# Thresholded attention on one core: scores in seven single PSUM banks, 512-column exponentials and copies on two engines, and an order of steps from a table

## The chip, the cores and the metric

The kernel runs on 1 core of one Trainium2 chip. The metric is device microseconds of one execution. PE, DVE, ACT, POOL and SP are the names of the core's engines as in the profile (TensorE, VectorE, ScalarE, GpSimd, SyncE); PEld is PE's loading of weights. PSUM is the memory into which PE writes; it has eight banks of 512 f32 columns on each of the 128 partitions.

## What is computed

The reference is attention with a cut (shapes: batch 8, heads 12, sequence 512, dimension 64, f32; threshold 0.1):

```
scores  = einsum('bhqd,bhkd->bhqk', Q, K) * scale
weights = exp(scores - max(scores)); weights /= sum(weights) + 1e-10
weights = where(weights > threshold, weights, 0)
weights /= sum(weights) + 1e-10
out     = einsum('bhqk,bhkd->bhqd', weights, V)
```

With these inputs most queries have no weight above 0.1, so their output row is zero, and the few others have one, so that their output row is one row of V.

## The kernel before, in words

The 96 heads are taken as 48 pairs (`hp`), two pairs make a unit (`q` or `u`, 24 of them; the first is split into two half units), and four units make a group (`x`, 6 of them).

**The coarse part** finds candidate queries. For each unit SP's queue loads K (`load_k`, L370 and after) and Q (`load_q`, L375), and writes zeros to the unit's part of the output (`do_zero`, L598). POOL scales Q and casts it to f16 (`do_qcast`, L385). PE transposes K in f32 (`do_ktr`, L395) and Q in f16 (`do_qtr`, L406) into PSUM. ACT copies K transposed out (`do_kev`, L413), POOL casts that to f16 (`do_kh`, L418), and DVE copies Q transposed out (`do_qev`, L422). Then, for each pair and each of four blocks `t` of 128 keys, PE makes scores of both heads, 128 x 1024 (`do_sc`, L438): this is a score step, of which there are 192. One engine, ACT with an exponential (L447) or DVE with an integer trick that stands for one (L449), turns them into an `e` tile (`do_ex`). PE sums `e` and a power of it over the keys into one accumulator bank, `acc` (`do_g`, L469; two such steps for a pair), and adds a bound from the sizes of the inputs, which DVE prepares (`do_bits`, L428; `do_size`, L476).

**The exact part** of a group, once all its sums are in `acc`: DVE empties it (`do_evac`, L479), PE and DVE flag the candidate queries and give each a slot (`do_test` to `do_oh`, L485 to L505), PE makes the indices (`do_idx`, L515), POOL gathers up to 128 rows of Q by an indirect DMA (`do_gather`, L529), and splits them (`do_split`, L536). PE transposes the rows (`do_xtr`, L541) and multiplies them with K in f32 (`do_xqk`, L555), ACT takes the exponential with its sum (`do_xexp`, L561), DVE finds the key above the cut (`do_xkeep`, L570), POOL gathers that row of V (`do_gv`, L585) and scatters it to the output (`do_scatter`, L592). The exact part of a group runs amid the coarse part of the next one; that of the last group has none behind it. A check at the end (L707 to L733) decides whether a slow branch is taken; it isn't with these inputs.

**PSUM** is cut into three tiles `two` of two banks each, for scores and transposes, one bank `acc`, and one bank `one` for the exact part. A `two` tile is held from PE's first matmul into it to the end of the instruction that empties it.

**The order.** Every step is recorded in a `Plan` (L11) with the engines that may do it, a cost, a latency after it, a priority, and the buffers it takes and gives back. `Plan.order` (L24) puts the steps one after the other on a modelled clock, and with that settles which of ACT and DVE does each exponential and which buffer each step uses. The steps are then issued in this order (L724), and `keep` holds the instructions of an engine in it. Each engine works through its own queue in order, and so does each engine that issues DMAs: an instruction that waits holds up all behind it. Two such entries, for the scores and the exponential:

```
add(("sc", hp, t), {"PE": 0.23}, 0.2, [("qev", u), ("kh", u)], g - 3, ...
add(("ex", hp, t), {"ACT": 0.95, "DVE": 1.14}, 0.15, [("sc", hp, t)], g, ...
```

Of the kernel before, what the change touches and what calls it, by code (L numbers as in the profile page):

```python
# [3 lines left out]

# [5 lines left out]

class Plan:  # L11
# [3 lines left out]
    SWITCH = 0.06  # L15

    def __init__(self, pools):
        self.ops, self.ids, self.pools = [], {}, pools

    def add(self, name, engs, lat, deps, prio, fn, takes=(), gives=(), mode=None):  # L20
        self.ids[name] = len(self.ops)
        self.ops.append((name, engs, lat, list(deps), prio, fn, list(takes), list(gives), mode))

    def order(self):  # L24
        ops, ids = self.ops, self.ids
        n = len(ops)
        succ, need, ready_at = [[] for _ in range(n)], [0] * n, [0.0] * n
        for i, op in enumerate(ops):
            for d in op[3]:
                succ[ids[d]].append(i)  # L30
                need[i] += 1
        engines = {e for op in ops for e in op[1]}
        free_at = {e: 0.0 for e in engines}
        ready = {e: set() for e in engines}
        pe_mode = None
        idle = {p: [(0.0, b) for b in range(k)] for p, k in self.pools.items()}
        held = {}

        def offer(i):
            for e in ops[i][1]:  # L40
                ready[e].add(i)

        for i in range(n):
            if need[i] == 0:
                offer(i)

        def begin(i, e):
            t = max(ready_at[i], free_at[e])
            if e == "PE" and ops[i][8] and pe_mode and ops[i][8] != pe_mode:
                t = max(ready_at[i], free_at[e] + self.SWITCH)  # L50
            want = {}
            for pool, _ in ops[i][6]:
                want[pool] = want.get(pool, 0) + 1
            for pool, k in want.items():
                if len(idle[pool]) < k:
                    return None
                t = max(t, sorted(idle[pool])[k - 1][0])
            return t

        out = []  # L60
        while len(out) < n:
            best = None
            for e in sorted(engines):
                at = [(begin(i, e), i) for i in sorted(ready[e])]
                at = [(t, i) for t, i in at if t is not None]
                if not at:
                    continue
                t0 = min(t for t, _ in at)
                prio, t, i = min((ops[i][4], t, i) for t, i in at if t <= t0 + 0.06)
                if best is None or (t, prio) < best[:2]:  # L70
                    best = (t, prio, i, e)
            assert best is not None, "the plan is stuck"
            t, _, i, e = best
            name, engs, lat, deps, prio, fn, takes, gives, mode = ops[i]
            for x in engs:
                ready[x].discard(i)
            free_at[e] = t + engs[e]
            if e == "PE" and mode:
                pe_mode = mode
            for pool, key in takes:  # L80
                b = min(idle[pool])
                idle[pool].remove(b)
                held[pool, key] = b[1]
            for pool, key in gives:
                idle[pool].append((t + engs[e] + lat, held[pool, key]))
            out.append((t, i, e))
            for j in succ[i]:
                ready_at[j] = max(ready_at[j], t + engs[e] + lat)
                need[j] -= 1
                if need[j] == 0:  # L90
                    offer(j)
# [7 lines left out]
def kernel(  # L99
# [21 lines left out]
    GP = 8  # L121
# [235 lines left out]
    def at(pool, key):  # L357
        return plan.held[pool, key]
# [450 lines left out]
```

## Time and profile before

| | us |
|---|---|
| median of 3 runs (lowest, highest) | 229.33 (223.48, 230.46) |
| the profiled execution | 225.0 |
| its span, first to last instruction | 223.3 |
| outside the span | 1.7 |
| busy: PE, DVE, ACT, POOL | 172.4, 158.9, 135.8, 83.9 |
| mean granted TensorE clock | 0.94 of full speed |

The span is one profiled execution. Busy times leave out waiting. A row of groups reads: line, engine, operation, output tile, input tile, shapes, count, then busy us in all and the mean ns of one, then the idle time just before these instructions and what ended most of it. In a row of the order of time the first number is the start in us, the second the time that the (merged) instructions took, and square brackets hold the idle time just before and its releaser. A matmul row's time holds its way through the array, so rows of PE that follow closely overlap. The names `two`, `one`, `qk` and so on are the kernel's tiles with the buffer number left out.

### The profile page before, as it was taken

The page shows a single profiled execution, that of the slowest core. Times are in us where ns is not written, and L with a number is a line of the kernel's source. Part 1 is how long each engine was busy: PE and PEld are TensorE (multiplying, and loading weights), DVE is VectorE, ACT ScalarE, POOL GpSimd, SP SyncE. Part 2 cuts the span into 40 slices and gives each one's busy share as a digit, 9 for nine tenths or more (in the row PEclk, how much of TensorE's full clock was granted, in tenths as well). Part 3 has the DMA queues.
Part 4 walks back from the last instruction along what each step waited for, and adds up shares of the span by engine and source line. Part 5 has one row for each costly group of instructions (what it writes and reads, how often), then busy time and mean ns, then how long its engine had stood idle before and what let it go on. Part 6 is the DMA issues. An engine that isn't in the chain of part 4 may idle for free. (4 is left out here: it accounts for less than half of the span.)

```text
span 223.3 us, 5606 instructions
## 1 busy us (share of the span) xinstructions
PE 172.4 (77%) x2240; PEld 68.4 (31%) x2240; DVE 158.9 (71%) x246; ACT 135.8 (61%) x147; POOL 83.9 (38%) x130
## 2 busy tenths in 40 slices
PE   1498997985989996985898986798987998993330
PEld 0233333341233341331334432334432343222100
DVE  6259987983478897696497797487797897796030
ACT  2366886763478875575466676467677678780010
POOL 7644324462066415334236143246155403130211
PEclk9999999997699999999699999799999999999585
DMA  5999999899659898485785676684687000000000
GB/s 122 237 281 308 281 288 266 232 304 267 166 122 273 241 254 224 156 220 129 211 240 121 203 188 179 211 244 117 205 262 297 3 3 6 3 1 1 6 1 12
DMA packets 67438, 38.43 MB, mean 172 GB/s; under 512 B 51880, under 2 KB 64240, under 8 KB 67408
## 3 DMA queue, kind: packets, MB, share of 16 engines
q1 hardware_dynamic: 66832, 37.76, 60.6%
q8 instruction: 19, 0.31, 0.6%
q0 software_dynamic: 576, 0.27, 0.6%
q14 instruction: 11, 0.09, 0.1%
HBM read 25.56 MB, written 12.78 MB: 172 GB/s over the span
## 5 line engine op out<-in xcount | busy, mean ns | idle before, releaser
L447 ACT ACTIVATE e<-two 128x1024 f16<-128x1024 f32 x107 | 108.0, 1025 | 50.4 <-PE two L438 48.7
L449 DVE TENSOR_SCALAR e<-two 128x1024 int16<-128x1024 f32 x85 | 102.7, 1221 | 29.0 <-PE two L438 28.6
L438 PE MATMUL two<-qk 64*128 64x512 f16 x384 | 70.8, 398 | 21.3 <-ACT e L447 9.1
L469 PE MATMUL acc<-e,w_sum 128*32 128x512 f16 x384 | 59.1, 397 | 0.4 <-DVE e L449 0.4
L469 PE MATMUL acc<-e,w_pow 128*32 128x512 bf16 x384 | 59.1, 397 | 0.0
L385 POOL TENSOR_SCALAR qh<-q 128x512 f16<-128x512 f32 x48 | 30.7, 640 | 55.7 <-issue 29.7
L438 PEld LDWEIGHTS <-qk 64*128 64x128 f16 x384 | 20.0, 95 | 67.8 <-issue 57.4
L366 POOL CAST qk<-kt 128x1024 f16<-128x1024 f32 (+1 forms) x25 | 26.2, 1046 | 15.8 <-ACT kt L362 14.9
L362 ACT COPY kt<-two 128x1024 f32<-128x1024 f32 (+1 forms) x25 | 24.4, 977 | 7.5 <-PE two L395 7.5
L395 PE MATMUL two<-identity_f,k 64*128 64x64 f32 x384 | 18.7, 242 | 9.1 <-DMA k<-in_K_dram 7.1
L395 PEld LDWEIGHTS two<-identity_f,k 64*128 64x128 f32 x384 | 16.0, 152 | 17.5 <-issue 5.6
L469 PEld LDWEIGHTS <-w_sum 128*32 128x32 f16 x384 | 12.3, 96 | 22.5 <-issue 18.9
L364 DVE COPY qk<-two 128x1024 f16<-128x1024 f16 (+1 forms) x25 | 16.5, 660 | 3.6 <-PE two L406 3.6
L428 DVE TENSOR_SCALAR v<-qk 128x1024 int32<-128x1024 int32 x24 | 17.9, 745 | 0.2
L555 PE MATMUL one<-kt,xq 128*32 128x512 f32 x96 | 14.7, 742 | 0.4 <-ACT xq L362 0.4
L529 POOL DMA_INDIRECT qs<-in_Q_dram,idx x6 | 6.8, 1127 | 21.6 <-DVE ix L524 21.5
L592 POOL DMA_INDIRECT out_dram<-vr,idx x6 | 6.2, 1028 | 21.6 <-PE two L438 6.1
L469 PEld LDWEIGHTS <-w_pow 128*32 128x32 bf16 x384 | 12.2, 96 | 0.0
L566 DVE TENSOR_SCALAR sums<-sums 128x1 f32<-128x1 f32 x6 | 0.9, 152 | 14.9 <-ACT xe L561 14.9
L585 POOL DMA_INDIRECT vr<-in_V_dram,idx x6 | 6.5, 1076 | 12.9 <-DVE oks L716 6.5
L406 PEld LDWEIGHTS <-qh 64*128 64x128 f16 x384 | 9.5, 98 | 5.6 <-issue 3.3
L406 PE MATMUL two<-identity_h,qh 64*128 64x64 f16 x384 | 10.3, 194 | 0.5 <-DVE e L449 0.3
(88 smaller groups left out, 81.9 us busy)
## 6 DMA issues: line engine op xcount, KB each, us to landing
k<-in_K_dram SPq DMA_DIRECT2D x96, 128.0 KB, 4.1
out_dram<-zero SPq DMA_DIRECT2D x24, 512.0 KB, 5.1
q<-in_Q_dram SPq DMA_DIRECT2D x23, 512.0 KB, 5.2
q<-in_Q_dram SPq DMA_DIRECT2D x2, 256.0 KB, 4.3
qs<-in_Q_dram,idx POOLq DMA_INDIRECT x6, 3.0
vr<-in_V_dram,idx POOLq DMA_INDIRECT x6, 3.5
out_dram<-vr,idx POOLq DMA_INDIRECT x6, 2.8
```

Of the source, the lines that this page charges most:

```text
L362: keep(nc.scalar.copy(dst, src))
L364: keep(nc.vector.tensor_copy(dst, src))
L366: keep(nc.gpsimd.tensor_copy(dst, src))
L385: keep(nc.gpsimd.tensor_scalar(dst, src, ALPHA, 1.0, op0=ALU.mult, op1=ALU.mult))
L395: keep(nc.tensor.matmul(dst[:, i, c:c + D], lhsT=src[ps, n0 + n, r, :], rhs=identity_f32[ps, ps], is_transpose=True, start=True, stop=True))
L406: keep(nc.tensor.matmul(dst[:, i, :].bitcast(f16)[:, c:c + D], lhsT=src[ps, n0 + n, r, :], rhs=identity_h[ps, ps], is_transpose=True, star ...
L428: keep(nc.vector.tensor_scalar(v_b[at("v", q)][:].rearrange("p a n c -> p (a n c)").bitcast(i32), qk_b[at("qk", q)][:].rearrange("p a n c ...
L438: keep(nc.tensor.matmul(dst[:, h, :], lhsT=qk[ps, 1, n, t * P:(t + 1) * P], rhs=qk[ps, 0, n, :], start=True, stop=True))
L447: keep(nc.scalar.activation(dst, src, ACTF.Exp, scale=math.log(2.0) / 1024.0, bias=exp_bias))
L449: keep(nc.vector.tensor_scalar(dst.bitcast(i16), src, EXP_BIAS * 1024.0, 0.0, op0=ALU.add, op1=ALU.max))
L469: keep(nc.tensor.matmul(dst[32 * j:32 * j + 32, :], lhsT=w, rhs=rhs, **turn(x, j)))
L555: keep(nc.tensor.matmul(one[at("one", ("xs", x))][32 * b:32 * b + 32, :], lhsT=xq[:, a * P + 32 * b:a * P + 32 * b + 32], rhs=kt_b[at("kt" ...
```

## The change

- PSUM is now seven single banks `bank` (pool `bk`) and `acc`. A score step, and a transpose of K or Q, takes two of the seven, one for each of its halves, and each half is given back by itself. The exact part's steps take one of the seven; its own bank `one` is gone.
- The exponential of a score step is two instructions of 512 columns, one for each head (`do_ex(eng, hp, t, h)`), and either engine may do either half. `do_g` picks its weights for each half by the engine that made it (`kind[hp, t, h]`).
- The copies of K transposed and of Q transposed are also two halves each, and each half may be done by ACT or DVE. Before, K's were all ACT's and Q's all DVE's. For the first half unit ACT and DVE also write the f16 keys straight from PSUM; POOL's cast does it for the others, as before.
- There are 14 `e` tiles instead of 12.
- `Plan.order` and all costs, latencies and priorities are gone. `Plan.run` issues the steps by a table of 1136 entries, each the number of a step, a letter for its engine, and the buffers that it takes.
- Q's first block is loaded through ACT's queue; all other loads stay on SP's.
- The last exact part has the same steps as before.

The diff, cut to its core:

```diff
+ORDER = """
+13A2 12S3 0G 11D 6G 5G 1D 38S 8G 10D 37S 7G 9G 64S2 14G1 2G 20P0.1 15P2.3 3G 18A3 16D9 4G 19A 21D 17A 22D 65S1
...
+    def run(self, table):
+        done = set()
+        for token in table.split():
+            no, eng, at = re.fullmatch(r"(\d+)([A-Za-z])(.*)", token).groups()
+            name, engs, deps, fn, takes, gives = self.ops[int(no)]
...
+            for pool, key, count in takes:
+                self.held[pool, key], got = got[:count], got[count:]
+            assert not got
+            fn(self.ENGINES[eng])
...
-    pools = {"two": 3, "acc": 1, "one": 1, "k": 4, "q": 3, "qh": 2, "kt": 10, "qk": 4, "v": 3, "e": 12,
+    pools = {"bk": 7, "k": 4, "q": 3, "qh": 2, "kt": 10, "qk": 4, "v": 3, "e": 14,
...
-    two = [psum.tile([P, 2, SO * P], f32, name=f"two{i}") for i in range(pools["two"])]
-    acc = [psum.tile([P, SO * P], f32, name=f"acc{i}") for i in range(pools["acc"])]
-    one = [psum.tile([P, SO * P], f32, name=f"one{i}") for i in range(pools["one"])]
+    bank = [psum.tile([P, SO * P], f32, name=f"bank{i}") for i in range(pools["bk"])]
+    acc = psum.tile([P, SO * P], f32, name="acc")
...
+        queue = nc.scalar if u == units[0] else nc.sync
...
-    def do_kev(eng, u):
+    def do_kev(eng, u, i):
         q, n0, k = u
-        src = two[at("two", ("ktr", u))][:, :, 0:k * SO * D].rearrange("p i (x c) -> p i x c", c=D)
-        copy(eng, halves(kt_b[at("kt", q)], n0, k), src)
+        src = bank_at(("kp", u), i)[:, 0:k * SO * D].rearrange("p (x c) -> p x c", c=D)
+        copy(eng, side(kt_b[at("kt", q)], n0, k, i), src)
...
-    def do_ex(eng, hp, t):
-        src = two[at("two", ("sc", hp, t))][:].rearrange("p h c -> p (h c)")
-        dst = e_b[at("e", (hp, t))][:].rearrange("p h c -> p (h c)")
+    def do_ex(eng, hp, t, h):
+        src, dst = bank_at(("sc", hp, t), h)[:], e_b[at("e", (hp, t))][:, h, :]
...
-                w = (w_sum, w_pow)[j // 2][kind[hp, t]][:, 31 - m:63 - m]
+                w = (w_sum, w_pow)[j // 2][kind[hp, t, j % 2]][:, 31 - m:63 - m]
...
-        add(("kev", u), {"ACT": 0.1 + 0.43 * k}, 0.15, [("ktr", u)], g0 - 9, lambda e, u=u: do_kev(e, u),
+            add(("kev", u, i), "ACT DVE", [("ktr", u)], lambda e, u=u, i=i: do_kev(e, u, i),
...
-        add(("qev", u), {"DVE": 0.05 + 0.28 * k}, 0.15, [("qtr", u), ("kh", u)], g0 - 7, lambda e, u=u: do_qev(e, u),
+            add(("qev", u, i), "DVE ACT", [("qtr", u)] + keys_of[:1], lambda e, u=u, i=i: do_qev(e, u, i),
...
-    for step, eng in plan.order():
-        step(eng)
+    plan.run(ORDER)
```

How the order moves, at three places. The number behind a tile's name is its buffer; the one behind the underscore only identifies the tensor.

ACT amid group 1, before: `two0` to `two2` are the three PSUM tiles, and `e` the output of an exponential.

```order
L447 ACTIVATE e1_144<-two2_114 128x1024
L362 COPY kt7_133<-two1_113 128x2x8x64
L447 ACTIVATE e3_146<-two1_113 128x1024
L447 ACTIVATE e5_148<-two1_113 128x1024
L447 ACTIVATE e7_150<-two1_113 128x1024
L362 COPY kt8_134<-two0_112 128x2x8x64
L447 ACTIVATE e9_152<-two2_114 128x1024
```

ACT at a like place in the order of the change:

```order
L467 ACTIVATE e7_153<-bank5_117 128x512
L467 ACTIVATE e6_152<-bank3_115 128x512
L467 ACTIVATE e3_149<-bank1_113 128x512
L467 ACTIVATE e2_148<-bank6_118 128x512
L467 ACTIVATE e2_148<-bank5_117 128x512
L467 ACTIVATE e1_147<-bank3_115 128x512
L467 ACTIVATE e1_147<-bank0_112 128x512
L467 ACTIVATE e0_146<-bank4_116 128x512
```

Before, four instructions in a row empty `two1`; now a bank comes back to ACT at the earliest some rows later, and DVE empties others in between.

POOL around the gather of V rows (`vr`, from V) and the scatter (`out`) of group 2, before: `qh` is a Q cast, `qk` a key cast, x2 two instructions.

```order
L366 CAST qk3_139<-kt5_131 128x1024
L585 DMA vr2_175<-in_V_dram,idx2_164 128x64
L592 DMA out_0_dram<-vr2_175,idx2_164 24576x64
L385 TENSOR_SCALAR qh0_124<-q0_121 128x512 x2
L366 CAST qk0_136<-kt6_132 128x1024
```

The same place in the change, and then the same of group 1:

```order
L403 TENSOR_SCALAR qh1_128<-q2_126 128x512 x2
L604 DMA vr0_178<-in_V_dram,idx0_167 128x64
L383 CAST qk2_141<-kt2_131 128x1024
L611 DMA out_0_dram<-vr0_178,idx0_167 24576x64
L403 TENSOR_SCALAR qh0_127<-q1_125 128x512 x2
L383 CAST qk1_140<-kt9_138 128x1024
```

```order
L604 DMA vr1_179<-in_V_dram,idx1_168 128x64
L611 DMA out_0_dram<-vr1_179,idx1_168 16384x64
L403 TENSOR_SCALAR qh1_128<-q0_124 128x512
L383 CAST qk2_141<-kt6_135 128x1024
L403 TENSOR_SCALAR qh1_128<-q0_124 128x512
L403 TENSOR_SCALAR qh0_127<-q2_126 128x512 x2
```

A key cast has moved in between the gather and its scatter in group 2 (the same in group 3; in group 0 two casts); in group 1 the scatter still follows its gather, as all of groups 1 to 4 did before.

POOL at the start, before: `row_no` is a constant of the exact part, `key_i` one of its key numbers; the test constants stand ahead of these rows.

```order
L292 CAST row_no_105<-row_i_104 128x8
L385 TENSOR_SCALAR qh0_124<-q0_121 128x512
L366 CAST qk0_136<-kt0_126 128x512
L299 IOTA key_i_106 128x512
L385 TENSOR_SCALAR qh0_124<-q0_121 128x512
```

In the change:

```order
L307 CAST row_no_105<-row_i_104 128x8
L318 CAST key_no_107<-key_i_106 128x512
L403 TENSOR_SCALAR qh1_128<-q2_126 128x512
L253 MEMSET test_f_96 128x48
L256 AFFINE_SELECT test_f_96<-test_f_96 128x8 x2
```

The first Q cast now has the key numbers ahead of it and the test constants behind it, and no key cast of the first half unit follows it.

More of the change, by code (lines that the diff above doesn't have):

```diff
@@ L206, with const @@
     later = {}
-    def const(name, t):
+    def const(name):
         def wrap(fn):
-            later[name] = (t, fn)
+            later[name] = fn
             return fn
```

423 lines of the change are left out of this document (212 added, 211 removed).

## The prediction

> **What bounds the kernel now.** I read the busy times by stage first. The three stages are the start (to the first score matmul), the body, and the exact step of the last group, which has nothing left to hide behind; below them stand one steady stretch and the three worst ones. Columns: window, length, busy us and instructions of PE, PE's weight loads, DVE, ACT and POOL, the granted clock, the DMA share, GB/s.
>
> ```profile
> 0.00:9.26 9.26, 1.60 (x25) 1.34 (x26) 4.12 (x32) 2.46 (x3) 6.66 (x36) 1.00 0.67 164
> 9.26:202.34 193.08, 165.22 (x2177) 65.11 (x2177) 149.80 (x195) 132.41 (x141) 73.76 (x91) 0.96 0.68 191
> 202.34:223.30 20.96, 5.61 (x39) 1.97 (x39) 5.02 (x19) 0.96 (x3) 3.50 (x4) 0.68 0.02 5
> 20.00:40.00 20.00, 17.74 (x261) 7.05 (x260) 17.33 (x19) 15.90 (x17) 6.87 (x10) 1.00 1.03 282
> 50.00:60.00 10.00, 7.11 (x43) 1.62 (x42) 3.40 (x5) 4.13 (x6) 1.78 (x4) 0.66 0.92 246
> 104.00:112.00 8.00, 4.94 (x66) 2.03 (x64) 3.66 (x5) 3.66 (x4) 3.37 (x5) 0.79 0.56 161
> 138.00:146.00 8.00, 5.41 (x68) 2.29 (x68) 4.11 (x5) 3.98 (x4) 3.43 (x6) 0.79 0.55 171
> ```
>
> The span is 9.3 + 193.1 + 21.0 = 223.3 us. In the body DVE and ACT together work 149.8 + 132.4 = 282.2 us, 141.1 each, 73% of the time. Between 20 and 40 us they do (17.33 + 15.90) / 20 = 1.66 us of work per us. By that rate the last three rows hold 4.5, 4.4 and 4.9 us of work in 10, 8 and 8 us: **three holes** that lose 5.5 + 3.6 + 3.1 = 12.2 us. The other 180.9 us of the body leave each of the two engines 180.9 - 141.1 = 39.8 us idle. What they wait for stands in the table of waits (us in total, times, longest):
>
> ```profile
> ACT e L447 <- PE two L438: 48.7, 69, 3.9
> DVE e L449 <- PE two L438: 28.6, 42, 2.8
> ```
>
> Both wait for scores. Two different reasons show in the order of time. The first, on ACT:
>
> ```profile
> 61.34 1.01 ACT L362 COPY kt<-two 128x1024 f32<-128x1024 f32 x1
> 62.89 1.02 ACT L447 ACTIVATE e<-two 128x1024 f16<-128x1024 f32 x1 [0.54 <-PE two L438]
> 64.45 1.02 ACT L447 ACTIVATE e<-two 128x1024 f16<-128x1024 f32 x1 [0.54 <-PE two L438]
> 66.01 1.02 ACT L447 ACTIVATE e<-two 128x1024 f16<-128x1024 f32 x1 [0.54 <-PE two L438]
> ```
>
> These are rows 40 to 43 of ACT's order, and all four read two1. PE can't refill the tile before ACT has left it, so each costs 1.02 us of work and a **round trip of 0.54 us**. The second reason, a hole, starts on POOL (the last row is PE's):
>
> ```profile
> 96.39 1.09 POOL L585 DMA_INDIRECT vr<-in_V_dram,idx  x1 [0.65 <-DMA k<-in_K_dram]
> 103.59 1.02 POOL L592 DMA_INDIRECT out_dram<-vr,idx  x1 [6.10 <-PE two L438]
> 104.68 1.31 POOL L385 TENSOR_SCALAR qh<-q 128x512 f16<-128x512 f32 x2
> 106.06 1.04 POOL L366 CAST qk<-kt 128x1024 f16<-128x1024 f32 x1
> 107.15 0.39 PE L438 MATMUL two<-qk 64*128 64x512 f16 x2 [3.06 <-POOL qk L366]
> ```
>
> The scatter sits 6.1 us at the head of POOL's queue. Behind it stand a Q cast and the key cast that PE's next scores need, so PE idles 3.06 us. The releaser that the row names is PE work; the gather of V rows just ahead, which the scatter writes out, is the likelier one.
>
> **The change part by part. Shorter instructions.** By these rows a half costs more than half:
>
> ```profile
> L447 ACT ACTIVATE e<-two 128x1024 f16<-128x1024 f32 x107 | 108.0, 1025 | 50.4 <-PE two L438 48.7 <-issue 0.7 <-DVE marks L489 0.2
> L449 DVE TENSOR_SCALAR e<-two 128x1024 int16<-128x1024 f32 x85 | 102.7, 1221 | 29.0 <-PE two L438 28.6
> L362 ACT COPY kt<-two 128x1024 f32<-128x1024 f32 x23 | 23.3, 1011 | 1.7 <-PE two L395 1.7
> L362 ACT COPY kt<-two 128x512 f32<-128x512 f32 x2 | 1.2, 587 | 5.8 <-PE two L395 5.8
> L364 DVE COPY qk<-two 128x1024 f16<-128x1024 f16 x23 | 15.7, 681 | 0.0
> L364 DVE COPY qk<-two 128x512 f16<-128x512 f16 x2 | 0.8, 425 | 3.6 <-PE two L406 3.6
> L489 DVE TENSOR_TENSOR marks<-one,limits 128x192 bf16<-128x192 f32 x6 | 2.1, 351 | 0.6 <-PE one L485 0.4
> L501 DVE TENSOR_TENSOR keys<-one,marks 128x64 bf16<-128x64 f32 x6 | 1.3, 217 | 0.5 <-PE one L497 0.5
> ```
>
> On ACT, 512 columns are worth 1.011 - 0.587 = 0.424 us, so a half exponential is 1.025 - 0.424 = 0.601. On DVE a column from PSUM in f32 takes (351 - 217) / 128 = 1.047 ns, 512 of them 0.536, so a half is 1.221 - 0.536 = 0.685. The built order has 231 halves on ACT and 153 on DVE: 138.8 + 104.8 = 243.6 us against 108.0 + 102.7 = 210.7 before, **+32.9 us**. The key copies: 24.5 us before; now 29 halves on ACT at 0.587, 17 on DVE at 0.685 (an f32 read, costed as the exponential), and the first two units' six quarter-size copies at about 0.4: 31.0, +6.5. The Q copies: 16.5 us before; now 29 halves on DVE at 0.425, 17 on ACT at 0.587, four small ones 1.3: 23.6, +7.1. Together +46.5 us; about 1 of it falls before the first scores, so the body holds 282.2 + 45.5 = 327.7, **164 us per engine** instead of 141. Nothing hides this: both engines are the ones that everything waits for. Its lower bound is about 160, if halves in a row overlap by some 0.02 us each.
>
> [...]
>
> **Seven single banks.** In the order before, 66 of the 242 instructions by which ACT and DVE empty score and transpose tiles read the same buffer as the last such instruction on their engine (37 and 29); in the new order it is 4 of 486. At 0.54 us, 62 x 0.54 = 33.5 us go, **16.7 per engine**. How much of the other idle time stays isn't shown by any row: at most all, 39.8 - 16.7 = 23.1; at least, I put 5. I take it from the steadiest stretch: from 20 to 40 us the two idle (2.67 + 4.10) / 2 = 3.4 of 20, which over 180.9 is 30.7; less 16.7 leaves **14**. The exact step's small matmuls lose their own bank and now hold one of the seven; fourteen e tiles instead of twelve cost no time.
>
> **The order on POOL.** From group 1 on, key casts mostly stand 7 to 11 score steps ahead of their first use (two of them 3 and 4), where they stood 3 to 6 ahead, and in three of the four groups with work behind them a cast stands between the row gather and its scatter, before in one. At 180 / 192 = 0.94 us per score step, 8 steps are 7.5 us, more than the 6.1 that the scatter sat. Only in group 1 does the scatter still follow its gather at once, with half a Q cast and the key cast behind it: 1.09 + 6.1 + 1.02 + 0.66 + 1.04 = 9.9 us against 7.5, so up to 2.4 late. In group 0 the row transpose gets some 5 us of ACT and DVE work behind the gather instead of 2 to 3. Of 12.2 us of holes I keep **1.5** (bounds 0 and 12.2). SP's queue keeps its bytes and puts the zero writes later; in 180 us the body would move 191 x 193.1 / 180 = 205 GB/s, below the 282 of 20 to 40 us.
>
> **The start.**
>
> ```profile
> 2.18 0.61 SPq L377 DMA_DIRECT2D q<-in_Q_dram  x1
> 5.51 0.62 POOL L385 TENSOR_SCALAR qh<-q 128x512 f16<-128x512 f32 x1 [0.42 <-DMA q<-in_Q_dram]
> 7.75 0.69 PE L395 MATMUL two<-identity_f,k 64*128 64x64 f32 x8 [2.54 <-DMA k<-in_K_dram]
> 8.20 0.45 PE L406 MATMUL two<-identity_h,qh 64*128 64x64 f16 x8
> ```
>
> Q's first block lands 3.3 us after its issue. On ACT's queue it is issued about 1.4 us earlier, at 0.8, so it lands near 4.1; POOL's constants ahead of the cast then end near 4.6 (1.65 us of test constants move behind it, 1.18 of key numbers ahead). PE no longer puts the second K block ahead of the first Q transposes: cast to 5.2, Q transposes to 5.7, K transposes to 6.4, copies to about 7.5. First scores at **7.6** instead of 9.26; at 8.4 if the load lands no earlier. ACT issues this one DMA ahead of its table load and has nothing else to do then.
>
> **Sum.** 7.6 + (164 + 14 + 1.5) + 21.0 = 208.1 us of span. The last group's steps are the same, so 21.0 stays. The profiled execution took 225.0 us, 1.7 more than its span: **209.8, so 210 us**. That execution lies near the fast end of the three runs (223.48 to 230.46, median 229.33); a change under 2% is about what a measurement of this kernel can't tell from none.
>
> **The rivals.** (1) *PE sets the pace.* It is busy 165.2 us in the body and gets the same matmuls; from 20 to 40 us it is at 17.74 of 20. If the waits outside the round trips are PE's, all 23.1 stay: 7.6 + 188.6 + 22.7 = 219. Against it: PE waited only 9.1 us for ACT to free a tile:
>
> ```profile
> PE two L438 <- ACT e L447: 9.1, 14, 1.0
> ```
>
> which says that PE was rarely held up, so this rival is a real one. (2) *The holes stay*, since POOL still waits in order for its gathers: 7.6 + (164 + 14 + 12.2) + 22.7 = 220.5. (3) *PE's clock falls in the body.*
>
> ```profile
> 108.00:110.00 2.00, 2.00 (x26) 1.22 (x26) 1.48 (x2) 0.98 (x2) 0.00 (x0) 0.50 1.01 325
> 142.00:144.00 2.00, 2.00 (x26) 1.01 (x22) 1.24 (x2) 1.52 (x2) 0.00 (x0) 0.50 0.98 358
> ```
>
> At half clock ACT and DVE got 5.22 / 4 = 1.31 us of work per us, 79% of 1.66. If PE pauses for the two slower engines so often that a quarter of the body, 45 us, runs so, that is 12 us more: 222. Against it: PE's pauses from 20 to 40 us left the clock at 1.00, and the drops shown follow idle stretches of about 3 us. [...] (4) *Slower: the fixed cost decides.* If ACT and DVE, with every piece half as long, keep the busy share of the body outside its holes, 141.1 / 180.9 = 78%, because each piece still ends in a wait on PE, the body is 164 / 0.78 + 1.5 = 212 and the time 242. It is slower by 2% from a body of 199, that is when 35 of the 39.8 us of waits come back. For it: 244 more PSUM reads, each with its own wait. Against it: the 66 round trips counted above.
>
> **How the numbers follow.** Forecast 0.50, PE's pace 0.17, holes 0.13, clock 0.06, fixed cost 0.14. Low end: 5 us of waits and no hole, 7.6 + 169 + 22.7 = 199, put at 200. High end 224, which takes in the first three rivals; what is left out is rival 4 and a little below. Faster by over 2%: the forecast, rival 1 and a third of rivals 2 and 3, 0.74; slower 0.14; the rest 0.12.
>
> **What would show it.** Right: half exponentials near 0.60 and 0.69 us; waits of ACT and DVE for scores at some 30 us in total, not 77; first scores before 8 us; no stretch of 8 us with under 5 us of work on each of the two; clock 1.00 from 10 to 190 us; the tail again 21 us. Wrong: a body above 190 us, from waits that stay at over 23 us per engine, or a hole behind a scatter.

## The result, and the profile after

Before: 227.46 us median of four runs (223.48 to 230.46). After: **203.80 us** (202.29 to 204.83, four runs). The ratio is **0.907, 95% interval 0.894 to 0.920**. Ratios not said to be on medians compare only executions within 1.5% of their kernel's fastest, so they differ a little from ratios of the medians (203.80 / 227.46 = 0.896). The forecast was 210 us, in a range of 200 to 224. The sum came out 6 us high, but three of its terms were off by 4 to 17 us and happened to cancel.

The stages of the profiled execution after (204.83 us, span 203.1), cut as in the prediction, then the steady stretch and the four stretches with least work. Columns: window, length, busy us and instructions of PE, PEld, DVE, ACT and POOL, granted clock, DMA share, GB/s.

```profile
0.00:7.91 7.91, 0.88 (x17) 0.80 (x18) 4.38 (x34) 2.21 (x4) 6.60 (x35) 1.00 0.70 176
7.91:180.89 172.98, 158.38 (x2185) 64.99 (x2184) 149.63 (x286) 144.84 (x291) 76.41 (x91) 0.96 0.76 214
180.89:203.10 22.21, 6.06 (x39) 1.92 (x39) 5.02 (x19) 0.95 (x3) 3.83 (x5) 0.57 0.02 5
20.00:40.00 20.00, 18.62 (x287) 7.86 (x286) 19.10 (x35) 19.30 (x39) 8.17 (x11) 1.00 0.97 261
48.00:56.00 8.00, 6.32 (x65) 1.92 (x66) 3.00 (x6) 3.20 (x9) 1.64 (x3) 0.79 1.03 269
64.00:72.00 8.00, 5.61 (x74) 2.15 (x74) 4.44 (x9) 4.73 (x10) 4.61 (x6) 0.79 1.05 281
136.00:144.00 8.00, 5.33 (x97) 2.35 (x95) 5.06 (x12) 5.99 (x12) 3.39 (x4) 0.95 0.95 339
144.00:152.00 8.00, 6.47 (x55) 2.19 (x57) 3.98 (x8) 2.69 (x6) 2.17 (x3) 0.62 0.36 144
```

Read it in the prediction's order. In the body DVE and ACT work 149.63 + 144.84 = 294.5 us, **147.2 each**; before it was 141.1, and 164 was forecast. The steady stretch gives (19.10 + 19.30) / 20 = 1.92 us of work per us, where before had 1.66. At that rate the four stretches below lose 4.8 + 3.2 + 2.2 + 4.5 = 14.7 us, and one more at 96 to 104 us (13.13 us of work in 8) loses 1.2: **15.9 us of holes**, not 1.5. The rest of the body leaves each engine 172.98 - 15.9 - 147.2 = **9.9 us of other waits**, where 14 were forecast. The start is 7.91 (forecast 7.6) and the tail 22.2 (21.0). The differences, -16.8 + 14.4 - 4.1 + 0.3 + 1.2 = -5.0, are those between the forecast span of 208.1 and the measured 203.1. How the idle time is shared between holes and other waits hangs on the rate: by before's 1.66, which the prediction used, the same five stretches lose 12.2 us, as much as before's holes did, and 13.6 are other waits.

The groups of exponentials, and the waits for scores (us in total, times, longest):

```profile
L467 ACT ACTIVATE e<-bank 128x512 f16<-128x512 f32 x231 | 121.8, 622 | 16.6 <-PE bank L459 15.7
L469 DVE TENSOR_SCALAR e<-bank 128x512 int16<-128x512 f32 x153 | 97.6, 682 | 5.8 <-PE bank L459 5.3
```

```profile
ACT e L467 <- PE bank L459: 15.7, 20, 4.4
DVE e L469 <- PE bank L459: 5.3, 6, 1.7
PE bank L560 <- POOL qb L555: 11.0, 4, 4.3
```

The waits fell from 48.7 + 28.6 to 15.7 + 5.3 us. And the group rows hold a trap: on ACT 231 x 0.622 = 143.7 us, but the busy time is 121.8; on DVE 153 x 0.682 = 104.3 against 97.6. The busy time counts each moment once, so instructions that follow each other **overlap**. In the order of time, first after, then before; columns: start, length of the run of instructions, and its count behind the x:

```profile
174.44 5.73 ACT L467 ACTIVATE e<-bank 128x512 f16<-128x512 f32 x11
176.79 3.28 DVE L469 TENSOR_SCALAR e<-bank 128x512 int16<-128x512 f32 x5
```

```profile
193.57 4.00 ACT L447 ACTIVATE e<-two 128x1024 f16<-128x1024 f32 x4 [0.30 <-PE two L438]
196.04 4.77 DVE L449 TENSOR_SCALAR e<-two 128x1024 int16<-128x1024 f32 x4 [0.24 <-PE two L438]
```

In these runs a half takes 5.73 / 11 = 0.521 us on ACT and 0.656 on DVE, though each shows 0.622 and 0.682. Two halves (1.04 and 1.31) cost little more than one whole (1.00 and 1.19). The runs still hold short waits: record by record in the traces, where the next starts with no wait, the medians from one start to the next are 0.48 and 0.60 for a half (after), 0.92 and 1.14 for a whole (before).

The worst hole, at 141 to 151 us, and what leads to it, on POOL, PE and ACT (the number in brackets is the idle time just ahead of the row):

```profile
137.19 1.12 POOL L548 DMA_INDIRECT qs<-in_Q_dram,idx  x1 [2.75 <-DVE ix L543]
145.07 0.40 POOL L555 TENSOR_TENSOR qb<-qs,ix 128x128 f32<-128x128 f32 x1 [4.27 <-DMA qs<-in_Q_dram,idx]
145.53 0.47 PE L560 MATMUL bank<-identity_f,qb 128*128 128x128 f32 x1 [4.20 <-POOL qb L555]
146.64 1.58 ACT L467 ACTIVATE e<-bank 128x512 f16<-128x512 f32 x3 [4.42 <-PE bank L459]
```

```profile
136.41 5.49 SPq L618 DMA_DIRECT2D out_dram<-zero  x5
```

```profile
148.00:150.00 2.00, 2.00 (x16) 0.51 (x12) 1.92 (x4) 0.22 (x1) 0.00 (x0) 0.50 0.02 4
DMA to landing us min/median/max: 2.6/4.3/7.8
```

A gather of query rows is issued at 137.2 and its rows are there at 145.0, 7.8 us later (the slowest of six, last line); SP issues five writes of zeros from 136.4 to 141.9. POOL's split, PE's transpose and ACT stand one behind the other, and PE comes back at half clock (0.50 at 148 to 150 us). The 16 f32 matmuls of the exact part then take 3.24 us; at 89 us, with the clock at 1.00, they took 1.92:

```profile
147.32 3.24 PE L574 MATMUL bank<-kt,xq 128*32 128x512 f32 x16
89.00 1.92 PE L574 MATMUL bank<-kt,xq 128*32 128x512 f32 x16
```

The hole at 48 us is of the same kind: PE's transpose stands behind a gather of query rows that took 5.9 us. Those at 64 and 96 us are of the kind that the prediction described: POOL's scatter stands behind a gather of V rows, landed after 6.6 us (58.2 to 64.8) and 4.7 (93.2 to 97.8). In the first of them PE's next transposes wait for the Q cast behind the scatter:

```profile
49.68 0.33 PE L560 MATMUL bank<-identity_f,qb 128*128 128x128 f32 x1 [1.86 <-POOL qb L555]
65.03 1.10 POOL L611 DMA_INDIRECT out_dram<-vr,idx  x1 [2.85 <-DMA k<-in_K_dram]
66.88 0.29 PE L424 MATMUL bank<-identity_h,qh 64*128 64x64 f16 x8 [1.82 <-POOL qh L403]
98.73 1.02 POOL L611 DMA_INDIRECT out_dram<-vr,idx  x1 [4.45 <-PE bank L459]
```

### The profile page after: what moved, and what is told of

Read it like the earlier page. It is cut to its first block, busy times and chain, and to the rows that moved or that the text cites. A ratio compares the mean times of both kernels' runs of the same rounds, so it can differ in the third digit from the quotient of the medians.

```text
span 203.1 us, 5841 instructions
## 1 busy us (share of the span) xinstructions
PE 165.3 (81%) x2240; PEld 67.7 (33%) x2240; DVE 159.0 (78%) x339; ACT 148.0 (73%) x298; POOL 86.8 (43%) x129
## 5 line engine op out<-in xcount | busy, mean ns | idle before, releaser
L467 ACT ACTIVATE e<-bank 128x512 f16<-128x512 f32 x231 | 121.8, 622 | 16.6 <-PE bank L459 15.7
L469 DVE TENSOR_SCALAR e<-bank 128x512 int16<-128x512 f32 x153 | 97.6, 682 | 5.8 <-PE bank L459 5.3
L459 PE MATMUL bank<-qk 64*128 64x512 f16 x384 | 66.9, 392 | 4.8 <-DVE qk L381 1.3
L383 POOL CAST qk<-kt 128x1024 f16<-128x1024 f32 (+1 forms) x24 | 25.7, 1073 | 33.0 <-ACT kt L379 15.9
L488 PEld LDWEIGHTS <-w_sum 128*32 128x32 f16 x384 | 14.1, 96 | 27.9 <-issue 23.1
L413 PE MATMUL bank<-identity_f,k 64*128 64x64 f32 x384 | 18.8, 238 | 0.5 <-ACT e L467 0.5
L413 PEld LDWEIGHTS bank<-identity_f,k 64*128 64x128 f32 x384 | 16.3, 148 | 6.5 <-DVE e L469 2.4
L379 ACT COPY kt<-bank 128x512 f32<-128x512 f32 (+1 forms) x30 | 17.3, 601 | 1.3 <-PE bank L413 1.1
L574 PE MATMUL bank<-kt,xq 128*32 128x512 f32 x96 | 16.3, 811 | 0.4 <-ACT xq L379 0.4
L381 DVE COPY kt<-bank 128x512 f32<-128x512 f32 (+1 forms) x20 | 12.6, 643 | 3.7 <-ACT qk L379 2.0
L611 POOL DMA_INDIRECT out_dram<-vr,idx x6 | 6.3, 1044 | 16.8 <-PE bank L459 5.7
L381 DVE COPY qk<-bank 128x512 f16<-128x512 f16 (+1 forms) x31 | 11.9, 406 | 1.9 <-PE bank L424 1.5
L424 PEld LDWEIGHTS <-qh 64*128 64x128 f16 x384 | 8.2, 96 | 13.5 <-POOL qh L403 9.5
L379 ACT COPY qk<-bank 128x512 f16<-128x512 f16 (+1 forms) x19 | 10.7, 589 | 1.9 <-PE bank L424 1.9
```

Of the source, the lines that this page charges most:

```text
L379: keep(nc.scalar.copy(dst, src))
L381: keep(nc.vector.tensor_copy(dst, src))
L383: keep(nc.gpsimd.tensor_copy(dst, src))
L413: keep(nc.tensor.matmul(bank_at(("kp", u), i)[:, c:c + D], lhsT=src[ps, n0 + n, r, :], rhs=identity_f32[ps, ps], is_transpose=True, start= ...
L424: keep(nc.tensor.matmul(bank_at(("qp", u), i)[:].bitcast(f16)[:, c:c + D], lhsT=src[ps, n0 + n, r, :], rhs=identity_h[ps, ps], is_transpos ...
L459: keep(nc.tensor.matmul(bank_at(("sc", hp, t), h)[:], lhsT=qk[ps, 1, n, t * P:(t + 1) * P], rhs=qk[ps, 0, n, :], start=True, stop=True))
```

## The experiments

Runs that show the same time of before were made on one chip, beside the same executions of the kernel before.

| run | what | us (lowest to highest) | before | ratio, 95% |
|---|---|---|---|---|
| e1 | before, split on the same engine | 229.10 (228.07 to 231.94) | 226.62 | 1.010 (1.001 to 1.020) |
| e2 | after, no zeros | 190.97 (190.55 to 192.17) | 226.62 | 0.845 (0.838 to 0.852) |
| e3 | after, last zeros behind | 201.18 (198.17 to 202.34) | 226.62 | none given |
| e4 | after, first Q on SP | 203.78 (201.02 to 205.70) | 226.62 | 0.904 (0.896 to 0.911) |
| e5 | seven banks, greedy order | 205.43 (200.37 to 207.47) | 225.64 | none given |
| e6 | six banks, greedy | 219.45 (217.51 to 223.03) | 225.64 | 0.976 (0.949 to 1.003) |
| e7 | before, no zeros | 212.10 (211.34 to 212.93) | 225.64 | 0.948 (0.933 to 0.963) |
| e8 | after, zeros gated | 201.17 (198.53 to 203.29) | 225.64 | 0.900 (0.868 to 0.933) |
| e9 | six banks and one, greedy | 212.19 (209.80 to 213.63) | 228.51 | 0.924 (0.916 to 0.933) |
| e10 | as e9, in pairs | 210.99 (210.54 to 211.84) | 228.51 | 0.926 (0.920 to 0.932) |
| e11 | as e5, planned for late gathers | 201.17 (196.50 to 204.95) | 228.51 | none given |
| e12 | as e10, same engine | 218.59 (217.31 to 218.76) | 227.41 | 0.961 (0.956 to 0.965) |

Where no ratio is given, the runs of that kernel lie too far apart for an interval (4 to 8.5 us between lowest and highest), and a difference of a few us is not told from none.

### What a half costs: e1

```diff
-            keep(nc.scalar.activation(dst, src, ACTF.Exp, ...))
+            for c in (slice(0, 512), slice(512, 1024)):
+                keep(nc.scalar.activation(dst[:, c], src[:, c], ACTF.Exp, ...))
```

(and the same for VectorE's form)

> The kernel before with one edit: each of the 192 exponentials of 1024 columns is issued as two of 512 on the same engine, one behind the other. Tiles, order of steps, loads and queues are those of before. Theory A (two halves in a row overlap their fixed part, as the rows of after let one think: five on ScalarE in 2.56 us, four on VectorE in 2.68 us): the two engines' work grows by 0 to 6 us together, and the time stays within 1% of before (226 to 230 us). Theory B (the prediction's sum: each half pays its own fixed part, 0.60 and 0.69 us each): the two engines get 33 us more work, 16 on each, and the time goes to 238 to 245 us. If the time falls below 224 us, splitting by itself is part of the gain, by a way that neither theory has.

The groups of e1:

```profile
L448 ACT ACTIVATE e<-two 128x512 f16<-128x512 f32 x214 | 114.2, 600 | 48.5 <-PE two L438 46.9 <-ACT e L448 0.4 <-issue 0.3
L451 DVE TENSOR_SCALAR e<-two 128x512 int16<-128x512 f32 x170 | 108.0, 683 | 28.6 <-PE two L438 28.1
```

and three of its rows on ACT, to be read beside the prediction's three at 62.89 to 66.01:

```profile
62.49 1.09 ACT L448 ACTIVATE e<-two 128x512 f16<-128x512 f32 x2 [0.48 <-PE two L438]
64.12 1.08 ACT L448 ACTIVATE e<-two 128x512 f16<-128x512 f32 x2 [0.54 <-PE two L438]
65.74 1.09 ACT L448 ACTIVATE e<-two 128x512 f16<-128x512 f32 x2 [0.54 <-PE two L438]
```

The duration of one half is 0.600 and 0.683 us, the prediction's 0.601 and 0.685. But 192 more instructions brought 114.2 + 108.0 - 210.7 = 11.5 us of work on the two engines, 0.06 us each, not 33 us, and 2.5 us of time on medians (interval 0.1 to 2.0% of before). A pair of halves takes 1.09 us where the whole took 1.02: the second starts 1.09 - 0.60 = 0.49 us after the first. Theory B falls. A is nearer, though its 0 to 6 us of work was too little.

The round trip of 0.54 us is unchanged. Splitting alone gives nothing; something else in the change does.

### What makes the waits go: e5, e6, e9, e10, e12

These five kernels are the changed one with another table. It is made by the rule of the kernel before (the step that can begin first, by priority), with the costs of halves. They differ in the buffers and engines that the rule may use; the PSUM tiles are single banks in all five, so on the chip each bank comes free by itself in each of them. One piece of each table; a token is the number of a step, its engine's letter, and the buffers it takes:

```diff
 after:  23P4.5.13 39G 26P2.6.12 105S1 24D 25A 44P0.1 27A 28D
+e5:     23P6.0.0 26P1.3.1 9G 65S1 24A 25D 29P2.4.2 39G 27A 28D
+e6, e9: 23P0.1.0 26P3.2.1 9G 65S1 24A 25D 29P4.5.2 39G 27A 28D
+e10:    23P0.1.0 26P2.3.1 9G 65S1 24A 25D 29P4.5.2 39G 27A 28D
+e12:    23P0.1.0 26P2.3.1 9G 65S1 24A 29P4.5.2 27D 39G 25A 28D
```

(Steps 24 and 25 are the two halves of the scores that step 23 makes. In e12 both are ACT's, and 27 and 28 both DVE's. e6 and e9 begin alike: in e9 the exact steps take a bank of their own.)

> The changed kernel (seven single banks, halves on either engine, first Q on ScalarE's queue) with another table: its steps are put in order by the rule by which the kernel before does it (the step that can begin first, by priority), with the costs of halves, and not by a search. Theory E (single banks and halves make the gain): the time stays within 3% of after, 201 to 209 us. Theory F (the searched order makes it): the waits of ScalarE and VectorE for scores come back, from 21 us together to over 50, and the time is 213 to 228 us. The holes behind the gathers are expected in both.

> As the run with the greedy table, but with six single banks for the scores and the transposes, the same amount of PSUM as the three tiles of two banks that the kernel before has. If it is the granularity that counts (a bank comes free after half an exponential pair and any free bank will do), six banks cost under 3 us against seven: 202 to 211 us. If it is the seventh bank, the time rises by over 5 us, and the waits of ScalarE and VectorE for scores rise by over 10 us together.

> As the run with the greedy table, but the eight PSUM banks are divided as in the kernel before: six for the scores and the transposes (single ones here), one kept for the exact steps, one for the sums. Theory E1 (what counts is that a bank comes free alone, after its own half): the time is within 3 us of the greedy table with seven shared banks, 203 to 209 us. Theory E2 (what counts is the number of banks that scores can take, and the one that stood idle most of the time is the gain): it lies at 214 to 221 us, near the run with six and no bank of their own for the exact steps (219.5).

> As the run with six banks and one, but planned so that banks go in three fixed pairs, and a pair is taken again only when both its halves have been read; the two halves of a tile still go to either engine (to both in 157 of 192 tiles). Against the kernel before with split exponentials (229.1 us) only the engines of the halves, the first loads and the buffers for exponentials differ. If the use of both engines on one tile is worth something by itself, it lies 6 us or more below that, at 212 to 223 us; if only single banks bring the gain, it stays at 224 to 232 us.

> As the run with six banks in pairs (211.0 us, 0.926 of before), with one rule more: the two halves of a tile go to the same engine, one behind the other (114 tiles to ScalarE, 78 to VectorE). This is the kernel before with split exponentials (1.010 of before) except for the halves of K and Q copies on either engine, the first loads, the number of buffers for exponentials, and a greedy order made with the costs of halves. Theory K (a tile is read by both engines at once, so its banks are back in half the time: that is the gain): 220 to 229 us, 0.96 to 1.01 of before, and ScalarE's and VectorE's waits for scores rise from 40 to over 60 us together. Theory L (the copies in halves, the buffers or the order made with the right costs bring it): 209 to 214 us, 0.92 to 0.94 of before.

Waits for scores, first of e12, then e10, e9 and e5:

```profile
ACT e L465 <- PE bank L457: 30.4, 47, 4.7
DVE e L467 <- PE bank L457: 16.8, 28, 1.2
```

```profile
ACT e L465 <- PE bank L457: 25.1, 33, 2.0
DVE e L467 <- PE bank L457: 15.0, 15, 2.3
```

```profile
ACT e L465 <- PE bank L457: 27.0, 33, 2.4
DVE e L467 <- PE bank L457: 15.7, 15, 3.0
```

```profile
ACT e L465 <- PE bank L457: 10.6, 16, 2.7
DVE e L467 <- PE bank L457: 17.0, 16, 3.0
```

From before to after this makes a ladder. Beside each step stands how often, in the order as built, an engine's next score or transpose comes from the tile it has just emptied, counted as the prediction did but without the first half unit's copies in the runs with tables. In e12 a tile is its pair of banks; from e10 on, single banks are counted. The ratios of e5 and, for comparison with it, of after are also given on medians.

| step | ratio | waits for scores, us | same buffer |
|---|---|---|---|
| before | 1 | 77.3 | 66 |
| e1: split, nothing else | 1.010 | 75.0 | 66 |
| e12: tiles of single banks, greedy order with costs of halves, copies in halves, first Q on ACT, 14 `e` tiles | 0.961 | 47.2 | 44 |
| e10: a pair's halves to either engine | 0.926 | 40.1 | 7 |
| e9: planned with each bank free by itself | 0.924 | 42.7 | 5 |
| e5: one pool of seven banks | 0.910 on medians | 27.6 | 0 |
| after: the table of the change | 0.907; 0.896 on medians | 21.0 | 2 |

- **e12 to e10** changes one rule of the planning. The time falls by 7.6 us, with intervals well apart. 37 returns to the same tile go; at 0.54 us they would be 20.0 us, 10.0 per engine. They were cheaper: PE refills the first bank of a pair while its reader is still at the second, as in these rows of e12, where ACT's second half ends at 64.33 and PE's refill starts at 63.90:

```profile
63.25 1.08 ACT L465 ACTIVATE e<-bank 128x512 f16<-128x512 f32 x2 [0.30 <-PE bank L457]
63.90 0.37 PE L457 MATMUL bank<-qk 64*128 64x512 f16 x1 [0.52 <-ACT e L465]
```

  Record by record in the traces, the engines stand idle for 15.4 us just ahead of e12's 44 returns (0.35 each, and 19 of them have none) and for 1.1 us ahead of e10's 7: some 14 us less, 7 per engine, near the 7.6 of the time. That fits the round trip as the thing to count, and giving a pair's halves to two engines removes most of them here. The order of all steps moves with that rule, and that it has no part of the 7.6 us isn't shown. Theory K of e12 holds for this part only: 0.961 is the very edge of what it gave, 218.6 us lie just under its 220, and the waits stayed under the 60 us that it named.
- **e10 to e9** plans with single banks in place of pairs. Nothing moves that these runs could tell, and at 212.2 us e9 lies between the ranges of its two theories, so neither E1 nor E2 is borne out. What single banks are worth on the chip isn't tested by this step, since e10 and e12 have them too; they came in between e1 and e12.
- **e9 to e5** lets the exact part's bank join the pool. The waits for scores fall by 15 us, though ACT's waits for the exact part's `xq` and `xe` grow from 20.2 to 29.5 us; the medians go from 0.929 to 0.910 of before. e5's runs lie 7 us apart, so the size is open. **e6**, where the exact steps take their bank out of six and one of the eight is left unused, is at 0.976 of before against e9's 0.924, so a bank less does count there.
- **e5 to after**: greedy and searched order aren't told apart, 0.910 against 0.896 on medians with e5's runs 7 us apart. Theory F, with over 50 us of waits and 213 us or more, falls. Theory E's range holds (201 to 209 us), but that single banks make it isn't shown by that.
- **e1 to e12** bundles several edits, 10.5 us on medians and 28 of the 56 us by which the waits for scores fall from before to after: the largest step. The first scores come 1.9 us earlier in e12 (7.01 us against 8.94); 22 fewer round trips would be 22 x 0.54 / 2 = 5.9 us at e1's price, and those left are cheaper, by the rows above. Which of the edits brings how much wasn't taken apart, the single banks among them.

### What makes the holes: e2, e7, e3, e8, e11

```diff
     def do_zero(eng, q):
-        keep(nc.sync.dma_start(out=Oz[q], in_=zero[:]))
+        pass
```

(e2: in the changed kernel; e7: in the kernel before)

> The changed kernel without the writes of zeros to the output (it leaves the zeros out, so the rows that no query is chosen for are never written). Theory C (the holes stand where an indirect gather lands late because the loads and the zero writes are in flight with it): the gathers of the chosen queries land in about 2.5 us in place of 4.3 (median), ScalarE's and VectorE's long idle stretches shrink from about 16 us of lost time to under 9, and the time goes to 195 to 199 us. Theory D (the holes are made by the order on GpSimd and TensorE, whatever is in flight): gathers land sooner but the time stays at 202 to 205 us.

> The kernel before without the writes of zeros (it leaves the zeros out of the output). The same cut took 13 us from the changed kernel. Theory G (the traffic costs the kernel before as much, so the change's gain is the same with and without it): 212 to 217 us. Theory H (the kernel before, with 77 us of waits for scores on its two engines, has the slack that hides late gathers, and the change uncovered them): 221 to 227 us.

The body of e2, with the stretch that holds the same part of the work as the worst hole of after; and what its gathers and PE's wait for the split queries became:

```profile
8.00:167.50 159.50, 152.81 (x2185) 64.18 (x2182) 148.80 (x286) 144.38 (x291) 74.85 (x91) 1.00 0.62 153
128.00:136.00 8.00, 7.83 (x115) 3.05 (x118) 7.16 (x16) 7.19 (x15) 5.37 (x7) 1.00 0.32 89
```

```profile
DMA to landing us min/median/max: 2.5/3.5/5.0
PE bank L560 <- POOL qb L555: 5.0, 2, 4.1
```

The work is the same, 148.80 + 144.38 = 293.2 us. Each engine's idle time in the body is 159.5 - 146.6 = 12.9 us, where after had 172.98 - 147.2 = 25.7. **Nearly all of the 13 us are idle time**, and the clock stays at 1.00. Theory C holds against D, and the gain is larger than it gave (191 us, not 195 to 199), though the gathers land later than it gave (3.5 us, not 2.5). The kernel before, without its zeros, lost its holes too. Two of the prediction's three, which had some 0.9 and 1.0 us of work per us and now have over 1.5:

```profile
104.00:112.00 8.00, 7.47 (x110) 3.46 (x108) 6.97 (x12) 5.29 (x6) 2.76 (x3) 1.00 0.53 139
136.00:144.00 8.00, 6.87 (x108) 3.33 (x100) 7.21 (x11) 5.29 (x7) 2.91 (x4) 1.00 0.59 151
```

That took 11.7 us off before by the ratio (1 - 0.948, interval 8 to 15 us; 13.5 on medians), and about as much off after ((0.907 - 0.845) x 227 = 14.1). Theory G: the change neither uncovered the holes nor closed them. Without the writes' traffic these stretches have work, in either order; the prediction's reading of them, an order on POOL that the new table mends, was not enough. One smaller hole stays in e2, at 48 to 56 us (11.59 us of work in 8), behind the gather that took longest there, 5.0 us.

Is it the place of the writes, or their amount? Two kernels move them:

```diff
+    zero_late = consts.tile([P, 4 * SO * D], f32)
...
-        keep(nc.sync.dma_start(out=Oz[q], in_=zero[:]))
+        if q == 19:
+            keep(nc.gpsimd.memset(zero_late[:], 0.0))
+        keep(nc.sync.dma_start(out=Oz[q], in_=(zero_late if q > 18 else zero)[:]))
...
-927D1 967P3.6.4 762G 966A
+927D1 967P3.6.4 762G 926S 988S 1029S 1070S 1111S 966A
```

> The changed kernel with its last five writes of zeros, which SyncE issues from 136 to 142 us while the last group's gather is in flight, moved behind the last scatter's first stage (their zeros come from a second tile that GpSimd fills there, so that SyncE waits). The same bytes are written in the end. Theory C: the last group's gather, issued at 137 us and landing near 145, lands 3 to 5 us sooner, the hole from 140 to 152 us closes by 3 to 5 us, and the time falls to 198 to 201 us. Theory D: the hole stays, 202 to 205 us. If the moved writes reach into the end of the kernel instead, the time is over 205 us and the tail is longer than 22.3 us.

```diff
+    zero_g = [consts.tile([P, 4 * SO * D], f32, name=f"zero_g{i}") for i in range(2)]
...
+        x = min(q // GQ, NX - 2)
+        if q >= GQ and q == GQ * x:
+            keep(nc.gpsimd.memset(zero_g[x % 2][:], 0.0))
+        keep(nc.sync.dma_start(out=Oz[q], in_=(zero if q < GQ else zero_g[x % 2])[:]))
```

> The changed kernel with all the same bytes, but with each group's four writes of zeros from the second group on issued behind the scatter of the group before (their zeros come from two tiles that GpSimd fills there), so that none is in flight while a gather of chosen queries is; the last two groups' eight writes fall into the time after the loads have ended. Theory C (gathers that land late behind bulk traffic make the holes): landings of the gathers fall to a median of 3.5 us or less, and the time goes to 194 to 199 us, most of the 13 us that leaving the writes out brought. If the loads alone keep the gathers late, or if it is the amount of traffic and not its place, the time stays at 200 to 205 us.

Both came out at 201.2 us, some 2.6 us under after on paper, within what these runs can tell. In e3 the gather of the worst hole (the fourth of six, not the last group's, as the expectation has it) took 4.7 us instead of 7.8, landed by 141.1 instead of 145.0, and its hole shrank (13.16 us of work from 136 to 144 and 14.72 from 144 to 152, where after had 11.05 and 6.67), so for that one place theory C was right. In e8 the median landing is later than after's (5.5 us against 4.3), only the slowest is sooner (5.9 against 7.8):

```profile
DMA to landing us min/median/max: 2.6/5.5/5.9
```

But e8's gate didn't keep the writes away from the gathers. At least four of its first five gathers had a write in flight; with the one from 158.6 to 164.3 us, for instance, a write issued at 157.3 landed at 164.2, long after the last load was issued (134.2). So e8 doesn't part loads from writes. What the landing goes with in the traces, if loosely, is the rate of all transfers in the gather's own time. In after the six gathers took 5.9, 4.8, 3.8, 7.8, 2.6 and 2.6 us while 320, 253, 238, 356, 13 and 12 GB/s moved. With loads alone, in e2, the first five took 5.0, 3.1, 4.1, 3.8 and 2.6 us at 248, 211, 209, 144 and 13 GB/s; e8's first five took 4.4 to 5.9 us at 242 to 306 GB/s. With loads alone a gather is late too, 3.1 to 5.0 us against 2.6 at 13 GB/s. That writes placed elsewhere help as far as the rate beside the gathers falls is the author's estimate from these figures. By which path the rate acts, no run shows.

The other way is to leave the traffic and plan for it:

```diff
-    stage("gather", {"POOL": 1.1}, 1.6, ...
+    stage("gather", {"POOL": 1.1}, 5.5, ...
...
-    stage("gv", {"POOL": 1.05}, 1.6, ...
+    stage("gv", {"POOL": 1.05}, 5.5, ...
```

(the two latencies in the greedy rule that makes the table of e5; what ran is the table that comes out)

> As the run with the greedy table and seven banks (205.4 us), but the order is made with 5.5 us from a gather's issue to its landing in place of 1.6, so that GpSimd and TensorE are given other work between a gather and the steps that need it. Same bytes, same instructions. Theory I (the holes are steps placed ahead of data that land late, and GpSimd and TensorE, which work in order, stand behind them): TensorE's waits for the split queries fall from 11 to under 4 us and the time goes to 197 to 202 us. Theory J (the traffic delays the loads of K and Q themselves, or the landing varies too much to plan for): 203 to 208 us.

PE's wait for the split queries in e5 and in e11:

```profile
PE bank L558 <- POOL qb L553: 11.2, 5, 3.7
```

```profile
PE bank L558 <- POOL qb L553: 4.4, 2, 4.2
```

It falls from 11.2 to 4.4 us, in one execution of each, while the gathers land as late as in e5 (3.9 to 5.9 us against 4.2 to 5.4 for the first four). Theory I gave under 4 us and 197 to 202: the time is 201.17 us, 0.880 of before on medians against e5's 0.910. The runs spread over 8.5 us, so the size of the gain isn't shown. e11 has the lowest ratio on medians of the kernels that compute everything (after has 0.896); a change of two numbers in a plain greedy rule does no worse, as far as these runs tell, than the searched table. So an order can meet late landings, if it plans for them.

### What the second queue is worth: e4

```diff
-        queue = nc.scalar if u == units[0] else nc.sync
+        queue = nc.sync
...
-13A2 12S3 0G 11D 6G 5G
+12S3 13A2 0G 11D 6G 5G
```

> The changed kernel with the first block of Q back on SyncE's queue, behind the first block of K, instead of on ScalarE's. The rest of the order is that of after. If the start is worth what the prediction charged for it (first scores at 7.6 us and not at 9.26), the first scores come 0.5 to 1.4 us later than after's 7.91 us and the time grows by as much, to 204.3 to 205.5 us; that may lie within what three rounds can tell. If the prediction's other bound holds (the loads share the same rings, and the second queue brings nothing), nothing moves.

First Q cast on POOL and first scores on PE, after and e4:

```profile
5.04 0.62 POOL L403 TENSOR_SCALAR qh<-q 128x512 f16<-128x512 f32 x1
7.91 1.04 PE L459 MATMUL bank<-qk 64*128 64x512 f16 x4 [1.31 <-DVE qk L381]
```

```profile
5.59 0.62 POOL L403 TENSOR_SCALAR qh<-q 128x512 f16<-128x512 f32 x1 [0.64 <-DMA q<-in_Q_dram]
8.45 1.04 PE L459 MATMUL bank<-qk 64*128 64x512 f16 x4 [1.31 <-DVE qk L381]
```

The queue is worth 0.54 us at the first scores, the low end of what was expected; in the time, 0.904 against 0.907, it isn't seen. The other 0.8 us of the earlier start (9.26 to 8.45) come with the rest of the change, which wasn't taken apart.

## Why the prediction was right, and where it wasn't

- **Direction and size of the whole: right, partly by luck.** Work too high by 17 us, holes too low by 14, other waits too high by 4 (by the prediction's own rate of 1.66 us of work per us, holes 11 too low and other waits right).
- **"A half exponential is 1.025 - 0.424 = 0.601 ... Nothing hides this": the failed step for the work.** The duration was right to 0.02 us, and multiplying it by a count was wrong: neighbours hide a part of each other. The 384 halves were summed to 243.6 us and came to 121.8 + 97.6 = 219.4, 0.06 less for each, where the lower bound allowed 0.02. The row of before already had a trace of it: 107 x 1.025 = 109.7 against 108.0 busy. Together exponentials (8.7) and copies brought 12.3 us to the two engines' body work, not 45.5.
- **Round trips: the mechanism is borne out, the price and the cause in part.** The waits for scores went to 21 us, below the "some 30" given. 37 returns fewer brought 7.6 us where 0.54 us each would be 10.0, and e12's trace shows 0.35 each. Halves on either engine are what removes most of them there; planning with single banks in place of pairs brought nothing, and what single banks save on the chip was not separated.
- **"Of 12.2 us of holes I keep 1.5": failed.** 15.9 us stay. The prediction took the scatter at the head of POOL's queue for the cause and mended the order around it, for a V gather that lands as in before; in after V gathers took up to 6.6 us and POOL still stood. And its sum had no price for PE standing behind a late gather of query rows, which makes the holes at 48 and 141 us: it gave group 0's transpose some 5 us of other work, the gather took 5.9, and the fourth group's 7.8. Both hang on the landing, and that went with the traffic (in after 2.6 us at 13 GB/s, 7.8 at 356). Rival 2 (holes stay) is what happened; it came out at 204 and not at 220.5 because the work was smaller.
- **PE's pace (rival 1): not yet.** Outside the holes the two engines' waits fell to 9.9 us each. Without the zeros PE is busy 152.81 of 159.50 us, 96%: there it comes next.
- **The clock (rival 3): in the steady stretch, no.** It is 1.00 from 20 to 40 us, with seven banks in rotation. In the body it falls to 0.5 in three stretches, 51.1 to 54.5, 68.1 to 71.5 and 143.2 to 150.0 us, all in holes, so the "1.00 from 10 to 190" failed with them.
- **Fixed cost decides (rival 4): no.** ACT and DVE are busy 147.2 of 157.1 us outside the holes, 94%, where that rival kept 78%.
- **Start and tail: near.** 7.91 for 7.6; the tail is 1.2 us longer than before, which wasn't followed up.

## What to carry to other kernels

Price many small instructions by busy time over count, or by the distance from one start to the next in a run of them, not by the mean duration: here neighbours overlapped (halves on ACT started 0.48 us apart, and each showed 0.62). Where an engine waits out a round trip with the one that refills its buffer, count how often its next piece comes from the buffer just emptied; here, letting a second engine take half the piece brought 7.6 us. An order planned with pairs can still run with single buffers on the chip, so a run of such an order says nothing of what single buffers are worth. Plan an indirect gather with the landing it has under the kernel's own traffic (here up to 7.8 us, not the 1.6 assumed), and before mending an order around a hole, take the traffic away once and see whether the hole goes.

## What the runs showed of the hardware

- Reads of 512 f32 columns of PSUM in a row start every 0.48 us on ACT and 0.60 on DVE (medians in after's trace), though each is shown with 0.62 and 0.68.
- Indirect gathers of up to 128 rows landed after 2.6 us with 13 GB/s moving beside them, 3.8 to 4.8 with 238 to 253, 5.9 with 320 and 7.8 with 356 (after).
- PE's granted clock was 0.50 from 143.2 to 150.0 us, from within an idle stretch of 4.20 us (141.3 to 145.5) on, and 16 f32 matmuls took 3.24 us there instead of 1.92.
